# Expert rows fetched by indirect DMA and transposed, in place of one-hot products over a split copy of all tokens

## The chip, the core and the metric

The kernel runs on one core of a Trainium2 chip. The metric is the time of one execution on the device, in microseconds (us). A core has five engines that run their own instruction streams: TensorE (PE, matrix products; loading its stationary operand shows apart as PEld), VectorE (DVE), ScalarE (ACT), GpSimd (POOL) and SyncE (SP, which here only issues DMAs). Data moves between DRAM and the on-chip memory through 16 DMA engines that all queues share.

## The reference

The reference is a transformer-like block over 512 tokens of width 1024: RMS norm, an RWKV-7 mixer and a Mamba-2 mixer side by side, gates, an output projection `w_out` with a residual, then a mixture of experts and a last RMS norm. Only the mixture matters for this change:

```
h2 = rmsnorm(x, ffn_norm_g)
grp    = argmax(h2 @ w_rg + b_rg)                 # one of 4 groups
experts = top 2 of the 8 experts of that group    # 32 experts in all
hid = silu(h2[tok] @ w_gate[e]) * (h2[tok] @ w_up[e])
y[tok] += weight * (hid @ w_down[e])
out = rmsnorm(x + y, final_norm_g)
```

Each of the 32 experts has three float32 matrices of 2 MB. Every token goes to two experts, so there are 1024 token rows for all experts together.

## The kernel before

The mixers fill the first 1000 us or so and the change does not touch their code. After them comes the output projection, in eight steps `block(k)` / `turned(k)` of 128 columns. `turned` turns the result back to token rows, keeps it as `x2` (token in the partition) and also writes `th`: all tokens with the channel in the partition, split into a high part and a rest so that two fast products add up to full precision. The split takes one ACT pass and one DVE (once a POOL) pass per step. The last step is followed by the router: a chain of small DVE operations on the scores, with PE kept busy by 60 and then 24 transposes of the identity (`awake`).

The experts are taken in 8 groups of 4. An expert has 64 places (`CAP`), so a group has 256. `one_hot` compares, on DVE, each token's place with the 256 places of the group and so makes `oh` (second choice) and `sel` (both choices): a matrix of tokens against places. From it come three things on PE:

- `gather`: the group's token rows, channels in the partition (`xe`). For each of 8 channel pieces it multiplies `th` by `sel`: 4 token tiles times 2 parts, 8 products of 256 columns, 64 per group, and ACT copies each piece out of PSUM with the norm's gain.
- `scales`: the gate weights and norms of the places, 16 products of 4 columns each, read by DVE into `gsl`.
- `transposed`/`turned`: `sel` turned, for adding the results back (`combine`).

An expert is then `hidden` (16 products for gate and up, two column halves at a time; `between()` runs after the first 8), `turn` (4 transposes of the hidden values) and `down` (16 products), whose result ACT copies to `yy` and DVE splits. PE's order is written out by hand (`manual_schedule`), exactly as the loop over `groups` calls it: the next group's `one_hot` after its first expert, `scales` and `turned` after the second, the whole `gather` after the fourth. For group 0 the first half of the gather stands before the first expert, the second half in its `between()`, and `scales` after its `hidden`. The other engines' order follows from the order of the code by a scheduler.

Weights are read by `expert_weights`: six DMAs of 1 MB per expert, all on SP's queue, in the order gate, up, gate, up, down, down. They take 15 slots in turn (`wslot`): 2 in a pool that is free when the mixers end, 8 in one that is free soon after, 4 that take the memory of the projection's input, and 1 that opens after the router. A DMA into a used slot waits for the PE instruction that read the slot last, and the DMAs behind it on SP's queue wait with it.

At the end the last group is added, each of 4 token tiles is normalised and written out. Tokens beyond an expert's 64 places would run a loop at the end (`tc.If`); in the profiled execution it is not entered.

Of the kernel before, what the change touches and what calls it, by code (L numbers as in the profile page):

```python
# [17 lines left out]
T = 512  # L18
D = 1024
# [20 lines left out]
# TensorE's order in the two phases of streams: a letter is the next piece of that stream, a number before it  # L40
# how many pieces of projections come first
# [21 lines left out]
def hybrid_block(ctx: ExitStack, tc: tile.TileContext, a, out):  # L63
# [52 lines left out]
    # eye4[32 q + 8 d + h, i, c] = 1 where i = 4 c + d  # L116
# [42 lines left out]
    acs_d = dram.tile([SH, T], F32, name="acs_d")  # L159

# [552 lines left out]
    # twice the sigmoid is tanh + 1; the up projections are halved for it  # L713
# [6 lines left out]
    # gu takes acc in once both are gated  # L720
# [203 lines left out]
    gr = xp.tile([128, 2, TT, 2, 2], F32R, name="gr")  # L924
# [4 lines left out]
    th = xp.tile([128, 2, KT, TT, 128], F32R, name="th")  # L929
    NEXA, NEXB, NEXC, NEXD = 2, 8, 4, 1  # L930
# [24 lines left out]
    with tc.tile_pool(name="op", bufs=2, side="right") as op:  # L955
# [33 lines left out]
        def turned(k, xT):  # L989
# [22 lines left out]
            pk = ps.rearrange("p (t c k) -> p k t c", t=TT, k=KT)  # L1012
# [16 lines left out]
        # TensorE's clock stays up while the experts are chosen  # L1029
# [65 lines left out]
        gf = sm("gf", 2, TT, 2)  # L1095
        V.tensor_copy(gf[:, 0, :, 0], rst)
        G.memset(gf[:, 1, :, 0], 0.0)
# [16 lines left out]
    eps_ = moe.enter_context(tc.tile_pool(name="eps", bufs=1, space=PSUM))  # L1114
    sf = S0.rearrange("p e s -> p (e s)")
# [16 lines left out]

    def scales(o, sel, ne):
        pt = eps_.tile([128, 4, CAP], F32, name="pt", tag="pt", bufs=1)
        pf = pt.rearrange("p k c -> p (k c)")
        n = min(128, ne * CAP)
        gsl = mo.tile([128, EG], F32, name="gsl", tag="gsl", bufs=2)
        for p in range((ne + 1) // 2):
            for j, w in enumerate((sel, o)):
                for t in range(TT):  # L1140
                    PE.matmul(pf[0:n, 4 * p:4 * p + 4], w[:, t, 128 * p:128 * p + n],  # L1141
                              gr[:, j, t].rearrange("p i q -> p (i q)"), start=j == 0 and t == 0, stop=j == 1 and t == TT - 1)
        sc = mo.tile([128, 8], F32, name="sc", tag="sc")
        V.tensor_copy(sc[0:n, 0:4 * ((ne + 1) // 2)], pf[0:n, 0:4 * ((ne + 1) // 2)])
        for e in range(ne):
            rows, c = slice(64 * (e % 2), 64 * (e % 2) + 64), 4 * (e // 2)
            for i in range(2):
                V.tensor_tensor(gsl[64 * i:64 * i + 64, e:e + 1], pf[rows, c + i:c + i + 1], sc[rows, c + 2 + i:c + 3 + i], op=OP.add)
        return gsl
# [4 lines left out]
    def gather(sel, n, xe=None, ks=range(KT)):  # L1154
        if xe is None:
            xe = rows_tile(n)
        for k in ks:
# [5 lines left out]
        return xe  # L1163
# [7 lines left out]
    def hidden(group, ws, q, ss_, between=lambda: None):  # L1171
# [8 lines left out]
        if group.gsl is None:  # L1180
            group.scales()
# [44 lines left out]
    class Prepared:  # L1226
        def __init__(self, g):
            self.ne = groups[g]
            n = self.ne * CAP
            self.gsl = None  # L1230
            self.o, self.sel = one_hot(sf[:, 0:n], n, float(T * first_of[g]))

        def gather(self, ks):
            if ks[0] == 0:
                self.xe = rows_tile(self.ne * CAP)
            gather(self.sel, self.ne * CAP, self.xe, ks)

        def scales(self):
            self.gsl = scales(self.o, self.sel, self.ne)
# [16 lines left out]
    nxt.gather(range(KT // 2))  # L1256
# [12 lines left out]
    for g, ne in enumerate(groups):  # L1269
        cur, nxt = nxt, None  # L1270
        for q in range(ne):
            ws = expert_weights(first_of[g] + q)
            def between():
                if not pend:
                    cur.gather(range(KT // 2, KT))
# [11 lines left out]
            if g + 1 < len(groups):  # L1287
# [28 lines left out]
    # tokens past an expert's first CAP  # L1316
    most = nc.values_load(cnt[0:1, 0:1], min_val=0, max_val=2 * T)
    with tc.If(most >= CAP + 1):
        sx = mo.tile([128, CAP], F32, name="sx", tag="sx")
        V.tensor_scalar(sx, S0[:, 0], float(CAP), None, op0=OP.add)  # L1320
        with tc.For_i(0, NE, 1) as e:
# [8 lines left out]
            for b in range(1, T // CAP):  # L1330
                more = Overflow()
                more.o, sel = one_hot(sx, CAP, 0.0)
                more.gsl = scales(more.o, sel, 1)
                more.xe = gather(sel, CAP)
# [36 lines left out]
```

## Time and profile before

| | us |
|---|---|
| median of 3 runs | 1612.97 |
| lowest and highest run | 1611.62, 1616.58 |
| profiled execution, first to last instruction (span) | 1610.7 |
| PE busy in the span | 1512.8 (94%) |
| DVE, ACT, POOL busy | 906.0, 690.8, 236.5 |
| HBM read over the span | 298.60 MB |

The page gives no other time of the profiled execution than its span, which is 2.3 below the median of the runs. In the profile a line such as L1161 is a line of the kernel's file; a group of instructions is named by what it writes and reads (`gps<-sel,th` is the gather's product into a PSUM tile `gps`). PE's products overlap, so the mean of one is longer than the distance from one to the next. "ld" is the loading of the stationary operand.

### The profile page before, as it was taken

What the parts mean: (1) busy time and instruction counts of PE and PEld (TensorE: products, weight loads), DVE (VectorE), ACT (ScalarE), POOL (GpSimd) and SP (SyncE); (2) the same over time, 40 slices, a digit from 0 to 9 for tenths busy, and PEclk for the clock granted to TensorE, in tenths of its full rate; (3) what the DMA queues carried; (4) which work ended last, traced back from release to release, by engine and by line L of the source; (5) the groups of instructions that cost most, each with busy time, mean ns of one, the idle gap of its engine ahead of it and who ended that gap; (6) DMA issues with size and microseconds to landing.
All of it is one profiled execution on the core that took longest, in us unless ns stands there. A gap on an engine that the chain in (4) does not pass through costs nothing.

```text
span 1610.7 us, 22331 instructions
## 1 busy us (share of the span) xinstructions
PE 1512.8 (94%) x8510; PEld 1000.1 (62%) x8510; DVE 906.0 (56%) x1942; ACT 690.8 (43%) x1316; POOL 236.5 (15%) x223
## 2 busy tenths in 40 slices
PE   6988999999999999989898989999999999999995
PEld 5755766667766777767686767884454545544532
DVE  5688757887677845464565677434333343343334
ACT  6556566674746544545555654422221212212211
POOL 3122002220122000141313455000000000000001
PEclk9999999989999999999999999999999999999998
DMA  4321222212222323775655538749899999899991
GB/s 143 93 58 32 62 64 84 63 42 60 82 65 68 107 85 118 232 200 148 177 181 156 170 92 252 274 157 368 337 391 390 418 371 417 362 393 389 364 406 55
DMA packets 182612, 319.06 MB, mean 198 GB/s; under 512 B 10569, under 2 KB 141891, under 8 KB 156899
## 3 DMA queue, kind: packets, MB, share of 16 engines
q1 hardware_dynamic: 180131, 316.90, 55.2%
q8 instruction: 69, 1.13, 0.3%
q10 hardware_dynamic: 2368, 0.68, 0.2%
q14 instruction: 44, 0.36, 0.1%
HBM read 298.60 MB, written 18.94 MB: 197 GB/s over the span
## 4 chain that ended last, share of the span: by engine, by line
PE 52%; DMA 5%; DVE 4%; ACT 3%; POOL 2%; issue 2%; SPq 0%; ACTq 0%; DVEq 0%; POOLq 0%
PE pgu L1176 14%; PE pd L1201 7%; PE pin L150 5%; PE pin L152 5%; PE pin L151 5%; PE gps L1219 4%; PE gps L1161 4%; DMA er<-acs_d 2%; PE pt L1192 1%; DMA lt<-acs_d 1%; DMA gt<-g_d 1%; PE pt L1141 1%; DVE wl L135 1%; ACT wh L69 1%; POOL lt L796 1%
## 5 line engine op out<-in xcount | busy, mean ns | idle before, releaser
L150 PE MATMUL pin<-hh,wh 128*128 128x512 f32 x664 | 301.6, 454 | 11.7 <-ACT wh L69 7.7
L152 PE MATMUL pin<-hh,wl 128*128 128x512 f32 x664 | 271.6, 409 | 13.3 <-DVE wl L135 13.3
L151 PE MATMUL pin<-hl,wh 128*128 128x512 f32 x664 | 270.9, 408 | 0.8 <-DVE hl L229 0.8
L1176 PE MATMUL pgu<-we,xe 128*64 128x512 f32 x512 | 232.7, 597 | 0.0
L1177 PE MATMUL pgu<-we,xe 128*64 128x512 f32 x512 | 232.7, 597 | 0.0
L135 DVE TENSOR_TENSOR wl<-raw,wh 128x1024 fp32r<-128x1024 f32 x115 | 152.9, 1329 | 106.0 <-ACT wh L69 104.9
L69 ACT ACTIVATE wh<-raw 128x1024 fp32r<-128x1024 f32 x115 | 121.3, 1055 | 98.9 <-PE pin L151 82.0
L150 PEld LDWEIGHTS pin<-hh,wh 128*128 128x128 f32 x664 | 130.3, 196 | 49.6 <-issue 10.3
L152 PEld LDWEIGHTS pin<-hh,wl 128*128 128x128 f32 x664 | 129.8, 195 | 48.9 <-DVE wl L135 18.1
L151 PEld LDWEIGHTS pin<-hl,wh 128*128 128x128 f32 x664 | 131.1, 197 | 27.7 <-issue 5.3
L1176 PEld LDWEIGHTS pgu<-we,xe 128*64 128x64 f32 x512 | 66.1, 137 | 127.3 <-issue 123.9
L69 ACT ACTIVATE hid<-pgu,gsl 64x512 f32<-64x512 f32 x32 | 21.8, 681 | 280.4 <-PE pgu L1177 280.4
L1201 PE MATMUL pd<-we,hT 128*64 128x512 f32 x512 | 116.1, 593 | 1.2 <-DVE yy L1206 1.2
L1185 DVE SCALAR_TENSOR_TENSOR hid<-pgu,gsl,hid 64x512 f32<-64x512 f32 x32 | 24.2, 756 | 113.0 <-ACT hid L69 113.0
L150 PE MATMUL pin<-yh,wh 128*128 128x512 f32 x192 | 78.9, 411 | 7.5 <-ACT wh L69 3.3
L1201 PEld LDWEIGHTS pd<-we,hT 128*64 128x64 f32 x512 | 37.5, 137 | 73.8 <-issue 71.9
L1308 POOL TENSOR_SCALAR ss<-ss 128x1 f32<-128x1 f32 x4 | 2.4, 609 | 531.4 <-ACT y L69 531.4
L1221 DVE TENSOR_TENSOR x<-gps,x 128x512 f32<-128x512 f32 x128 | 78.1, 682 | 3.3 <-PE gps L1219 3.3
L1206 DVE TENSOR_TENSOR yy<-pd,yy 64x512 fp32r<-64x512 f32 x64 | 44.0, 687 | 63.4 <-ACT yy L69 62.5
L152 PE MATMUL pin<-yh,wl 128*128 128x512 f32 x192 | 76.7, 399 | 2.0 <-DVE wl L135 2.0
L69 ACT ACTIVATE yy<-pd 64x512 fp32r<-64x512 f32 x64 | 37.8, 591 | 89.8 <-PE pd L1201 88.9
L151 PE MATMUL pin<-yl,wh 128*128 128x512 f32 x192 | 76.1, 397 | 0.1
(365 smaller groups left out, 2675.8 us busy)
## 6 DMA issues: line engine op xcount, KB each, us to landing
we<-in_w_exp_gate_dram SPq DMA_DIRECT2D x64, 1024.0 KB
we<-in_w_exp_up_dram SPq DMA_DIRECT2D x64, 1024.0 KB
we<-in_w_exp_down_dram SPq DMA_DIRECT2D x64, 1024.0 KB
raw<-in_w_in_dram SPq DMA_DIRECT2D x83, 512.0 KB
lt<-acs_d SPq DMA_DIRECT2D x16, 512.0 KB
raw<-in_w_up_ssd_dram SPq DMA_DIRECT2D x16, 512.0 KB
xc_d<-cv SPq DMA_DIRECT2D x24, 256.0 KB
gt<-g_d SPq DMA_DIRECT2D x24, 256.0 KB
```

The costliest lines, as they stand in the source:

```text
L69: S.activation(o, i, f, **kw)
L135: V.tensor_tensor(lo, raw, hi.bitcast(F32), op=OP.subtract)
L150: PE.matmul(ps, wh[:, k, cs], xh[:, k], start=k == 0, stop=False)
L151: PE.matmul(ps, wh[:, k, cs], xl[:, k], start=False, stop=False)
L152: PE.matmul(ps, wl[:, k, cs], xh[:, k], start=False, stop=k == kt - 1)
L1161: PE.matmul(ps[:, 0:n], th[:, i, k, t], sel[:, t], start=i == 0 and t == 0, stop=i == 1 and t == TT - 1)
L1176: PE.matmul(pgu[0:64], xe[k // 4][:, k % 4, ss_], wg[k // 4][:, k % 4], start=k == 0, stop=k == KT - 1)
L1177: PE.matmul(pgu[SR], xe[k // 4][:, k % 4, ss_], wu[k // 4][:, k % 4], start=k == 0, stop=k == KT - 1)
L1201: PE.matmul(pd[i][64 * i:64 * i + 64], hT[:, k], wd[k // 2][:, k % 2, 512 * i:512 * i + 512], start=k == 0, stop=k == 3)
L1206: V.tensor_tensor(yy[i][rows, 1], src, yy[i][rows, 0].bitcast(F32), op=OP.subtract)
L1219: PE.matmul(ps, oT[0:n, 128 * t:128 * t + 128], yy[i][0:n, q], start=q == 0, stop=q == 1)
L1221: V.tensor_tensor(av, ps, av, op=OP.add)
```

## The change

The split copy `th` (32 KB per partition) is gone. In its place each step of the output projection writes its 128 columns of `x2` to a DRAM tensor `x2_d`, by a DMA on ACT's queue. `scales` multiplies by two more columns, of which one holds the token's number plus one, so that it yields for each place the token that sits there (or none). DVE turns that into an index list `at`. Two indirect DMAs on POOL's queue (`fetch`) then read the rows of 128 places each from `x2_d` into `xg`, one row of 4 KB per partition; places without a token have an index past the end and are left out. `gather` transposes `xg` on PE, 16 transposes of 128x128 per group in place of 64 products, and ACT copies as before. The memory of `th` becomes three more weight slots (`NEXA` 2 to 5, 18 in all) and the two `xg` tiles.

```diff
-    NEXA, NEXB, NEXC, NEXD = 2, 8, 4, 1
+    NEXA, NEXB, NEXC, NEXD = 5, 8, 4, 1
...
-            tk = [th[:, i, :, :, 16 * k:16 * k + 16] for i in range(2)]
-            act(tk[0], pk, AF.Copy)
             act(x2[:, :, ds_], ps.rearrange("p (t c) -> p t c", c=128), AF.Copy)
-            if k < KT - 1:
-                V.tensor_tensor(tk[1], pk, tk[0].bitcast(F32), op=OP.subtract)
-            else:
-                G.tensor_tensor(tk[1], x2[:, :, ds_].rearrange("p t (c k) -> p k t c", k=KT), tk[0].bitcast(F32), op=OP.subtract)
+            nc.scalar.dma_start(x2_d.rearrange("(t p) d -> p t d", p=128)[:, :, ds_], x2[:, :, ds_])
...
+        G.memset(gf[:, 1], 0.0)
+        G.iota(gf[:, 0, :, 2], pattern=[[128, TT]], base=1, channel_multiplier=1, allow_small_or_imprecise_dtypes=True)
...
+    xg = [mo.tile([128, D], F32, name=f"xg{p}") for p in range(2)]
+    for p in range(2):
+        G.memset(xg[p], 0.0)
...
+        tok = sc.rearrange("p (b q) -> p b q", q=6)[0:n, 0:np_, 2]
+        V.tensor_scalar(past[0:n, 0:np_], tok, 0.0, 4096.0, op0=OP.is_equal, op1=OP.mult)
+        V.scalar_tensor_tensor(at[0:n, 0:np_], tok, -1.0, past[0:n, 0:np_], op0=OP.add, op1=OP.add)
...
+    def fetch(at, ne):
+        n = min(128, ne * CAP)
+        for p in range((ne + 1) // 2):
+            G.indirect_dma_start(out=xg[p][0:n], out_offset=None, in_=x2_d,
+                                 in_offset=bass.IndirectOffsetOnAxis(ap=at[0:n, p:p + 1], axis=0),
+                                 bounds_check=T - 1, oob_is_err=False)
...
+    def gather(xe, ps_, n=128):
+        for k in range(KT):
             ps = ptile()
-            for i in range(2):
-                for t in range(TT):
-                    PE.matmul(ps[:, 0:n], th[:, i, k, t], sel[:, t], start=i == 0 and t == 0, stop=i == 1 and t == TT - 1)
-            act(xe[k // 4][:, k % 4], ps[:, 0:n], AF.Copy, scale=fgp[:, k:k + 1])
+            for i, p in enumerate(ps_):
+                PE.transpose(ps[:, n * i:n * i + n], xg[p][0:n].rearrange("p (c k) -> p k c", k=KT)[:, k], ident[0:n, 0:n])
+            act(xe[k // 4][:, k % 4, 128 * ps_[0]:128 * ps_[0] + n * len(ps_)], ps[:, 0:n * len(ps_)], AF.Copy,
+                scale=fgp[:, k:k + 1])
...
     nxt = Prepared(0)
-    nxt.gather(range(KT // 2))
+    nxt.fetch()
+    nxt.gather([0])
...
                 if not pend:
-                    cur.gather(range(KT // 2, KT))
+                    cur.gather([1])
                     return
...
                 if q == 1:
-                    nxt.scales()
+                    nxt.fetch()
                     nxt.turned()
                 if q == ne - 1:
-                    nxt.gather(range(KT))
+                    nxt.gather([0, 1])
```

On PE, between the router's `awake` (`rt<-ident`) and the first half of the first expert (`pgu`), the kernel before has the first half of the gather:

```order
L1033 MATMUL rt<-ident 128x128 x24
L1161 MATMUL gps<-sel,th 128x256 x32
L1176 MATMUL pgu<-we,xe 64x512
```

The changed kernel has the products of `scales` and then the transposes of the first fetched tile at that place:

```order
L1027 MATMUL rt<-ident 128x128 x24
L1140 MATMUL pt<-gr,sel 128x6 x4
L1140 MATMUL pt<-gr,oh 128x6 x4
L1140 MATMUL pt<-gr,sel 128x6 x4
L1140 MATMUL pt<-gr,oh 128x6 x4
L1170 MATMUL gps<-ident,xg_9375 128x128 x8
L1185 MATMUL pgu<-we,xe 64x512
```

So the 16 products of `scales`, the index list and a DMA now stand ahead of the first expert, where 32 products stood.

On POOL's queue, from the last operation of the output projection on, the kernel before has the last split of `th` and then nothing until the last norm (`ss`):

```order
L998 TENSOR_TENSOR rst<-rst,halfn 128x4
L1019 TENSOR_TENSOR th<-x_8729,th 128x32x16
L1308 TENSOR_SCALAR ss_12673<-ss_12673 128x1
```

The changed kernel has there two clears of `xg` and sixteen fetches, two per group, of which the first four are shown:

```order
L1112 MEMSET xg_9375 128x1024
L1112 MEMSET xg_9376 128x1024
L1158 DMA xg_9375<-x_d,at 128x1024
L1158 DMA xg_9376<-x_d,at 128x1024
L1158 DMA xg_9375<-x_d,at 128x1024
L1158 DMA xg_9376<-x_d,at 128x1024
```

The split left POOL, and the fetches have its queue to themselves.

On SP's queue, from the first weights of an expert on, the loads of `w_out` (`raw`) and of weights (`we`) stood in this order before:

```order
L951 DMA we<-in_w_exp_up_dram 128x2048
L131 DMA raw<-in_w_out_dram 128x8x128 x2
L951 DMA we<-in_w_exp_gate_dram 128x2048
L951 DMA we<-in_w_exp_up_dram 128x2048
L131 DMA raw<-in_w_out_dram 128x8x128
L951 DMA we<-in_w_exp_down_dram 128x2048
```

And they stand so in the changed kernel:

```order
L951 DMA we<-in_w_exp_up_dram 128x2048
L131 DMA raw<-in_w_out_dram 128x8x128
L951 DMA we<-in_w_exp_gate_dram 128x2048
L951 DMA we<-in_w_exp_up_dram 128x2048
L131 DMA raw<-in_w_out_dram 128x8x128
L951 DMA we<-in_w_exp_down_dram 128x2048
```

One load of `w_out` moved behind two loads of weights there; 14 weight loads are now in the queue ahead of the wait for the projection's last product, where 10 were.

## Rows read from the trace of the kernel before

**Rows 1.** The page: GB/s moved by DMA in 40 equal slices of the span.

```profile
GB/s 143 93 58 32 62 64 84 63 42 60 82 65 68 107 85 118 232 200 148 177 181 156 170 92 252 274 157 368 337 391 390 418 371 417 362 393 389 364 406 55
```

**Rows 2.** The page's DMA issues: what, queue, count, KB each.

```profile
we<-in_w_exp_gate_dram SPq DMA_DIRECT2D x64, 1024.0 KB
```

**Rows 3.** Windows: length, busy us (instructions) of PE, PEld, DVE, ACT, POOL, clock, DMA share, GB/s.

```profile
1300.00:1350.00 50.00, 50.00 (x263) 24.18 (x264) 18.32 (x40) 10.47 (x19) 0.00 (x0) 1.00 1.01 420
...
1450.00:1500.00 50.00, 50.00 (x267) 24.99 (x268) 16.64 (x35) 10.48 (x19) 0.00 (x0) 1.00 0.93 364
```

**Rows 4.** Chain of waits, 1075 to 1610, its longest pieces: start, us, what.

```profile
1328.29 7.86 PE gps L1161 x64
...
1521.51 7.86 PE gps L1161 x64
```

**Rows 5.** Waits of SP's queue, 960 to 1610: total us, times, longest.

```profile
SPq L951 <- PE pd L1201: 254.9, 50, 15.5
```

**Rows 6.** Waits of the engines, 1075 to 1610: total us, times, longest.

```profile
PEld pgu L1176 <- DMA we<-in_w_exp_down_dram: 0.7, 2, 0.4
```

**Rows 7.** Groups by line, 960 to the end: shapes, count, busy us, mean ns.

```profile
L1161 PE MATMUL gps<-sel,th 128*128 128x256 f32 x512 | 64.2, 285 | 0.2
...
L1192 PEld LDWEIGHTS pt<-ident,hid 64*128 64x128 f32 x128 | 17.7, 209 | 26.6 <-issue 25.1 <-PE pgu L1177 1.5
...
L69 ACT ACTIVATE xe<-gps,fgp 128x256 f32<-128x256 f32 x64 | 30.4, 475 | 34.8 <-PE gps L1161 34.7
```

**Rows 8.** Timeline at the gather of group 1: start, us, engine, line, what.

```profile
1135.02 7.93 PE L1161 MATMUL gps<-sel,th 128*128 128x256 f32 x64
1135.12 1.21 ACT L69 ACTIVATE yy<-pd 64x512 fp32r<-64x512 f32 x2 [2.73 <-PE pd L1201]
...
1142.88 0.64 PE L1176 MATMUL pgu<-we,xe 128*64 128x512 f32 x1
```

**Rows 9.** Timeline from the router to expert 0's scales.

```profile
1065.63 1.52 POOL L1019 TENSOR_TENSOR th<-x,th 128x512 fp32r<-128x512 f32 x1 [2.15 <-ACT x L69]
...
1066.08 1.21 DVE L1045 TENSOR_TENSOR f32A<-el,m 128x128 f32<-128x128 f32 x1
...
1068.94 0.29 DVE L1045 TENSOR_TENSOR f32A<-el,m 128x128 f32<-128x128 f32 x1
...
1074.83 0.88 DVE L1130 SCALAR_TENSOR_TENSOR sel<-S,idf,oh 128x256 fp32r<-128x256 f32 x2
...
1079.43 0.64 PE L1176 MATMUL pgu<-we,xe 128*64 128x512 f32 x1
...
1092.62 0.17 DVE L1144 COPY sc<-pt 128x8 f32<-128x8 f32 x1 [16.61 <-PE pt L1141]
```

**Rows 10.** Chain of waits, 950 to 1200: start, us, what.

```profile
976.44 2.75 DMA gt<-g_d
...
1083.09 4.03 PE gps L1161 x32
...
1090.70 1.89 PE pt L1141 x16
...
1107.27 0.95 PE gps L1168 x8
```

**Rows 11.** PE in short windows: length, PE busy (instructions), granted clock, DMA share, GB/s.

```profile
303.00:304.00 1.00, 0.00 (x0) 1.00 0.00 0
...
305.00:306.00 1.00, 1.00 (x5) 0.50 0.38 80
...
308.00:309.00 1.00, 1.00 (x5) 0.92 0.00 0
...
964.00:968.00 4.00, 2.10 (x10) 1.00 0.09 33
968.00:972.00 4.00, 3.26 (x15) 1.00 0.49 151
```

**Rows 12.** Groups of POOL over the whole span.

```profile
L534 POOL MEMSET TF<- 128x1024 f32 x8 | 8.3, 1043 | 109.0 <-PE cb L588 108.9
```

More of the change, by code (lines that the diff above doesn't have):

```diff
@@ L159, in hybrid_block @@
     acs_d = dram.tile([SH, T], F32, name="acs_d")
+    x2_d = dram.tile([T, D], F32, name="x2_d")
     x_in = a["x"][0]
@@ L923, in hybrid_block @@
     cnt = xp.tile([128, 1], I32, name="cnt")
-    gr = xp.tile([128, 2, TT, 2, 2], F32R, name="gr")
+    gr = xp.tile([128, 2, TT, 2, 3], F32R, name="gr")
     S0 = xp.tile([128, EG, CAP], F32, name="S0")
@@ L928, in hybrid_block @@
     nc.scalar.dma_start(fgp, a["ffn_norm_g"][0].rearrange("(p k) -> p k", k=KT))
-    th = xp.tile([128, 2, KT, TT, 128], F32R, name="th")
-    NEXA, NEXB, NEXC, NEXD = 2, 8, 4, 1
+    NEXA, NEXB, NEXC, NEXD = 5, 8, 4, 1
     ex = ctx.enter_context(tc.tile_pool(name="ex", bufs=NEXB, side="right"))
@@ L1135, in scales @@
         pf = pt.rearrange("p k c -> p (k c)")
-        n = min(128, ne * CAP)
+        n, np_ = min(128, ne * CAP), (ne + 1) // 2
         gsl = mo.tile([128, EG], F32, name="gsl", tag="gsl", bufs=2)
-        for p in range((ne + 1) // 2):
+        for p in range(np_):
             for j, w in enumerate((sel, o)):
                 for t in range(TT):
-                    PE.matmul(pf[0:n, 4 * p:4 * p + 4], w[:, t, 128 * p:128 * p + n],
+                    PE.matmul(pf[0:n, 6 * p:6 * p + 6], w[:, t, 128 * p:128 * p + n],
@@ L1142, in scales @@
                               gr[:, j, t].rearrange("p i q -> p (i q)"), start=j == 0 and t == 0, stop=j == 1 and t == TT - 1)
-        sc = mo.tile([128, 8], F32, name="sc", tag="sc")
-        V.tensor_copy(sc[0:n, 0:4 * ((ne + 1) // 2)], pf[0:n, 0:4 * ((ne + 1) // 2)])
+        sc = mo.tile([128, 12], F32, name="sc", tag="sc")
+        V.tensor_copy(sc[0:n, 0:6 * np_], pf[0:n, 0:6 * np_])
+        tok = sc.rearrange("p (b q) -> p b q", q=6)[0:n, 0:np_, 2]
+        past = mo.tile([128, 2], F32, name="past", tag="past")
@@ L1145, in scales @@
+        at = mo.tile([128, 2], I32, name="at", tag="at", bufs=2)
+        V.tensor_scalar(past[0:n, 0:np_], tok, 0.0, 4096.0, op0=OP.is_equal, op1=OP.mult)
+        V.scalar_tensor_tensor(at[0:n, 0:np_], tok, -1.0, past[0:n, 0:np_], op0=OP.add, op1=OP.add)
         for e in range(ne):
-            rows, c = slice(64 * (e % 2), 64 * (e % 2) + 64), 4 * (e // 2)
+            rows, c = slice(64 * (e % 2), 64 * (e % 2) + 64), 6 * (e // 2)
             for i in range(2):
-                V.tensor_tensor(gsl[64 * i:64 * i + 64, e:e + 1], pf[rows, c + i:c + i + 1], sc[rows, c + 2 + i:c + 3 + i], op=OP.add)
@@ L1149, in scales @@
-        return gsl
+                V.tensor_tensor(gsl[64 * i:64 * i + 64, e:e + 1], pf[rows, c + i:c + i + 1], sc[rows, c + 3 + i:c + 4 + i], op=OP.add)
+        return gsl, at
+    def fetch(at, ne):
[4 more added lines that the diff above has]
+                                 bounds_check=T - 1, oob_is_err=False)
@@ L1151, in rows_tile @@
     def rows_tile(n):
         return [wp.tile([128, KT // 2, n], F32, name="xe", tag="wh", bufs=2) for i in range(2)]
[L1154 to L1157, printed above, removed]
+    def gather(xe, ps_, n=128):
+        for k in range(KT):
             ps = ptile()
-            for i in range(2):
-                for t in range(TT):
-                    PE.matmul(ps[:, 0:n], th[:, i, k, t], sel[:, t], start=i == 0 and t == 0, stop=i == 1 and t == TT - 1)
-            act(xe[k // 4][:, k % 4], ps[:, 0:n], AF.Copy, scale=fgp[:, k:k + 1])
-        return xe
+            for i, p in enumerate(ps_):
+                PE.transpose(ps[:, n * i:n * i + n], xg[p][0:n].rearrange("p (c k) -> p k c", k=KT)[:, k], ident[0:n, 0:n])
+            act(xe[k // 4][:, k % 4, 128 * ps_[0]:128 * ps_[0] + n * len(ps_)], ps[:, 0:n * len(ps_)], AF.Copy,
+                scale=fgp[:, k:k + 1])
@@ L1179, in hidden @@
                 between()
-        if group.gsl is None:
-            group.scales()
         gsl = group.gsl[:, q:q + 1]
@@ L1229, in __init__, with fetch, gather @@
             n = self.ne * CAP
-            self.gsl = None
             self.o, self.sel = one_hot(sf[:, 0:n], n, float(T * first_of[g]))
-        def gather(self, ks):
-            if ks[0] == 0:
+        def fetch(self):
+            self.gsl, at = scales(self.o, self.sel, self.ne)
+            fetch(at, self.ne)
+        def gather(self, ps_):
+            if ps_[0] == 0:
                 self.xe = rows_tile(self.ne * CAP)
-            gather(self.sel, self.ne * CAP, self.xe, ks)
-        def scales(self):
-            self.gsl = scales(self.o, self.sel, self.ne)
+            gather(self.xe, ps_)
         def turned(self):
@@ L1332, in hybrid_block @@
                 more.o, sel = one_hot(sx, CAP, 0.0)
-                more.gsl = scales(more.o, sel, 1)
-                more.xe = gather(sel, CAP)
+                more.gsl, at = scales(more.o, sel, 1)
+                fetch(at, 1)
+                more.xe = rows_tile(CAP)
+                gather(more.xe, [0], CAP)
                 oT = turned_tile()
```

4 lines of the change are left out of this document (1 added, 3 removed).

## Prediction

> **What bounds the kernel now.** I read the page's slices first: from about 1080 us to the end PE is busy in every slice, at full clock, while DMA moves 360 to 420 GB/s [rows 1]. Two resources are thus near their limit, and the windows say which one leads: from 1300 to 1350 and from 1450 to 1500 PE is busy for 50.00 of 50 us, although the transfers ran at 420 GB/s in the one and at 364 in the other [rows 3]. PE sets the pace. The waits say it again: SP's queue, which issues the weights, waited 254.9 us for products that had yet to read a slot [rows 5], PE only 0.7 us for a weight [rows 6]. The chain of waits gives the period: two gathers that are three groups apart start at 1328.29 and 1521.51, so a group of four experts takes 193.22 / 3 = 64.41 us, of which the gather is one piece of 7.86 [rows 4]. In a period 24 loads of 1024 KB [rows 2] move 25.17 MB, that is 391 GB/s, against 420 where the queue was never out of slots [rows 3].
>
> So in this phase what leaves PE's stream comes off the time, until PE needs less per group than the transfers.
>
> **The gather of groups 1 to 7.** Removed are 64 products in 7.86 us of PE: the first product of the next expert comes at 1142.88, the gather began at 1135.02 [rows 8]. Added are 16 transposes of 128x128. The eight of L1168, of that shape, took 0.95 us [rows 10], 0.119 each, so PE itself needs 1.9 us; or 3.3 us if each is held by its stationary load read with a stride, as in L1192 (209 ns, at a smaller shape [rows 7]). But each pair fills a PSUM tile, there are three tiles, and ACT empties them with the copies it made before, 475 ns each [rows 7]. ACT is busy at that moment: two copies of `yy` run from 1135.12 for 1.21 us [rows 8], so its first copy of the gather starts at about 1136.35. The old products hid that; the transposes don't. With 0.49 us per copy (0.475 and a little between two), the eighth tile's transposes can start when the fifth copy has ended, at 1136.35 + 5 x 0.49 = 1138.8, and end at about 1139.1. The gather takes 4.1 us, and each group saves 3.7: 7 x 3.73 = **-26.1**. Bounds: if PE alone paced it, 5.9 saved per group, -41.7; if each copy costs 0.1 more for the hand-over between PE and ACT, a gather of 5.9 and 2.0 saved, -13.7. I take the middle value, which goes by the copies' own row.
>
> `scales` keeps its 16 products (six columns for four) and its place after the second expert, and `at` is ready some 26 us before the gather that uses it (one and a half experts of 16.1 us). A fetch of 0.5 MB has that long to land: nothing in groups 1 to 7, unless it is very late (a rival below).
>
> **The start, group 0.** Here nothing hides the fetch. Before: the two last `sel` tiles begin at 1074.83 and take 0.88, the gather's first half follows, and the first `pgu` starts at 1079.43 [rows 9]. After, step by step:
>
> - POOL's split at L1019 goes. Beside it one DVE step took 1.21 us, its like three steps later 0.29 [rows 9]: the router is 0.92 shorter and `sel` is done at 1074.8.
> - 13 of the 16 products of `scales` need the last `sel`: 13 x 1.89 / 16 [rows 10] = 1.5, to 1076.4.
> - DVE copies `sc`, makes `past` and `at`: three small steps of about 0.17 [rows 9] with hand-overs and what DVE has begun, together 1.2, to 1077.6.
> - POOL's two clears of `xg`, 1.04 each [rows 12], run beside the router's end; their cover is some 3 us, without it they cost up to 2.1.
> - The fetch. No indirect DMA is in this trace. Nearest is a direct load of 256 KB, 2.75 us from issue to landing [rows 10], against 256 KB of rows here. I take 3.5, to 1081.1; bounds 2 and 10.
> - Eight transposes and copies of 128 columns: ACT paces them, at most 0.475 less a little; 2.4 to the last copy that the first product wants.
>
> The first `pgu` comes at about 1083.5, +4.1. Given back: the gather's second half takes 2.4 in place of 4.03 (-1.6), and `scales` is gone from behind the first `hidden` (-1.9, both [rows 10]). That leaves +0.6. Then the clock: PE has nothing to do for some 5 us. [...] Some 3.5 us at half clock cost about 1.7. The start is **+2.3**; from -3 (short fetch, clock holds) to +10.
>
> **What costs nothing.** The removed ACT and DVE passes of the projection and the added writes of `x2_d` lie beside PE's products, which fill that stage; if the writes delayed it, it would be through their 2 MB of traffic, 5 us at 420 GB/s, beside transfers that have pauses there. I take 0, bounds -2 and +2. The order on SP's queue moves one load of `w_out` by two loads of weights; the same bounds. The last norm is untouched.
>
> **Does DMA keep up?** The fetches add 0.52 MB per group: 25.69 MB, 61.2 us at 420 GB/s, against 64.41 - 3.73 = 60.7 of PE. The two are level. The three added slots carry the difference: 18 loads are 45 us of transfers ahead of PE, of which about 25 are slots PE still reads (`down` is read an expert later), so about 20 us (an estimate) can be eaten over the phase, where 8 x 0.5 = 4 are needed. I take 0; without the slots it would be about +4.
>
> **Sum**, against the profiled execution (span 1610.7, the median of the runs 2.3 above): -26.1 + 2.3 = -23.8, a span of 1586.9 and a time of **1589**.
>
> [...] The row: a DVE step with two inputs in SBUF went from 0.29 to 1.21 us beside a POOL operation [rows 9]. [...]
>
> **The rivals.**
>
> *Deeper.* ACT's copies start at once or PE paces: -36 to -40, **1574**. For it: 1.9 us of PE's own work. Against: ACT's `yy` copies are in the way in each group. 0.08.
>
> *DMA becomes the bound.* The windows show 420 and 364, the latter with PE at 50 of 50 [rows 3], so it was waiting for slots, but nobody knows how much of it. If the sustained rate is 404, a group takes 63.6 us, 2.9 above PE; 8 x 2.9 - 20 = 3: **1592**. If 391 is all there is, 65.7, 8 x 5 - 20 = 20: **1609**. Against: 420 over 50 us. 0.17. [...]
>
> *The clock falls, or the start is long.* A fetch of 10 us or so at the start: +8, **1597**. Or the clock falls in every gather, since PE works for 1.9 of 4.1 us: 7 x 1.7 = 12, **1601**. Against the second: from 964 to 968 PE worked 2.10 of 4 us, and the clock stayed at 1.00 there and in the next 4 us [rows 11]. 0.15 together.
>
> *The fetch comes late, slower than before.* One mechanism: POOL makes the two fetches of a group slowly (row by row, or starved beside DVE, or in line behind 1 MB loads), and PE stands at the gather of each group until they land. From `at` to the gather there are 26 us; the gain of 24 is gone when a pair takes 26 + 24 / 7 = 29.4 us, and at 35 us it costs 7 x 9 = 63 less 24: **1652**. For it: no indirect DMA was seen here. Against: 256 KB took 2.75 us elsewhere [rows 10], ten times less. 0.07.
>
> *It doesn't do what it says:* transposes and copies in turn without overlap, 8 x (0.24 + 0.475 + hand-over) = 7 us and more, so the gather is as long as it was: about 0 and the start, **1614**. 0.06.
>
> **Numbers.** The forecast as described has 0.47. The range is 1577 to 1604: it takes in the bounds of the gather, the start and the milder half of DMA, and leaves out the deepest gain, 391 GB/s and the last two. A difference of 0.3%, 4.8 us, is what a measurement of this kernel can tell. Faster by more: forecast, deeper, clock and most of DMA, 0.86; within: part of DMA's, and of the last, 0.06; slower 0.08.
>
> **What would show it.** The gather on PE: about 4.1 us, waiting for `xe` copies, the first one behind `yy`. The distance between gathers of neighbouring groups: 60.7. The first `pgu` some 4 us later, with a granted clock of 0.5 shortly before or after it. Waits of PE for `xg` only at group 0. DMA at 0.95 to 1.0 with about 420 GB/s. I am wrong in the bound if PE waits for `we` by more than 5 us in all, in the fetch if any gather after group 0 waits for `xg`, and in the copies if the gather is under 3 or over 6 us.

## The result and the profile after

The changed kernel took 1595.68 us (median of 4 runs, 1592.07 to 1599.62), the kernel before 1614.78 in the runs beside it: a ratio of 0.9878, 95% interval 0.9847 to 0.9909. It is 19.1 us faster; 23.8 were forecast, and 1589 lies 6.7 below the time measured. The profiled execution has a span of 1590.4, 20.3 below the span before.

In the expert phase the same windows as in [rows 3] now read (length; busy us and instructions of PE, PEld, DVE, ACT, POOL; granted clock, DMA share, GB/s):

```profile
1300.00:1350.00 50.00, 49.07 (x226) 20.41 (x222) 20.53 (x37) 8.62 (x17) 1.59 (x2) 1.00 1.01 424
1450.00:1500.00 50.00, 50.00 (x236) 21.14 (x234) 19.51 (x40) 6.69 (x11) 1.99 (x2) 1.00 0.91 375
```

PE has short gaps now (0.93 us in the first window, one per gather; none in the second, which holds no gather). DMA moves 424 GB/s in the first, where it moved 420, and 375 in the second, where it moved 364; in the windows between them it is at 423 and 424. The gather of group 1, against [rows 8], in the timeline (start, us, engine, line, what; in brackets the idle time before it and what ended it):

```profile
1143.18 0.93 PE L1170 MATMUL gps<-ident,xg 128*128 128x128 f32 x6
1143.28 1.21 ACT L69 ACTIVATE yy<-pd 64x512 fp32r<-64x512 f32 x2 [2.73 <-PE pd L1208]
...
1144.52 3.03 ACT L69 ACTIVATE xe<-gps,fgp 128x256 f32<-128x256 f32 x8
1145.04 1.95 PE L1170 MATMUL gps<-ident,xg 128*128 128x128 f32 x10 [0.93 <-ACT xe L69]
1146.92 0.64 PE L1185 MATMUL pgu<-we,xe 128*64 128x512 f32 x1
```

Three pieces (six transposes) are done in 0.93 us, then PE waits for ACT, which copies `yy` until 1144.49 and only then the first piece. From 1143.18 to 1146.92 the gather takes 3.74 us, where it took 7.86. The last gather starts at 1504.98:

```profile
1504.98 0.93 PE L1170 MATMUL gps<-ident,xg 128*128 128x128 f32 x6
```

Six groups lie between them: (1504.98 - 1143.18) / 6 = 60.30 us per group, against 64.41.

The start looks worse than forecast. The timeline from the router to the first expert:

```profile
1068.78 6.71 PE L1027 MATMUL rt<-ident 128*128 128x128 f32 x60
...
1076.85 1.39 DVE L1127 TENSOR_SCALAR oh<-S,idf 128x256 fp32r<-128x256 f32 x2
1077.04 2.09 POOL L1112 MEMSET xg<- 128x1024 f32 x2 [8.19 <-DVE idf L1075]
...
1079.48 0.87 DVE L1128 SCALAR_TENSOR_TENSOR sel<-S,idf,oh 128x256 fp32r<-128x256 f32 x2
...
1082.82 0.16 DVE L1148 SCALAR_TENSOR_TENSOR at<-sc,past 128x2 int32<-128x2 f32 x1
...
1083.88 1.31 POOL L1158 DMA_INDIRECT xg<-x_d,at  x1 [4.74 <-DVE at L1148]
...
1087.62 2.66 PE L1170 MATMUL gps<-ident,xg 128*128 128x128 f32 x8 [5.61 <-DMA xg<-x_d,at]
...
1090.21 1.12 PE L1185 MATMUL pgu<-we,xe 128*64 128x512 f32 x1
```

Before, the router's keep-awake products began at 1064.22:

```profile
1064.22 7.55 PE L1033 MATMUL rt<-ident 128*128 128x128 f32 x60
```

The first `pgu` came at 1079.43 [rows 9], 15.21 us later; now it is 21.43.

And there is a loss ahead of the router that I had not forecast. In the first step of the output projection the waits of PE (total us, times, longest) show

```profile
PE plg L1000 <- DVE xT L986: 6.0, 1, 6.0
```

and the timeline of DVE, ACT's queue and SP's queue says why:

```profile
998.87 0.42 SPq L951 DMA_DIRECT2D we<-in_w_exp_up_dram  x1
...
1000.06 0.94 ACTq L970 DMA_DIRECT2D wr<-in_w_router_expert_dram  x1
...
1004.23 0.65 SPq L951 DMA_DIRECT2D we<-in_w_exp_down_dram  x1
...
1013.14 0.46 DVE L971 TENSOR_TENSOR wr<-wr,vec 128x288 f32<-128x288 f32 x1 [9.37 <-DMA wr<-in_w_router_expert_dram]
```

The router's weights `wr` (two small loads, whose rows are 16 and 128 bytes) need 13.1 us from issue until DVE can use them, while loads of 1 MB (`up` and `down` here, and a `gate` issued at 998.24) are on the engines with them. From 1004 to 1006 us the DMA view counts, for the queue of the weights (q1) and that of `wr` (q10), packets, MB and the share of the 16 engines:

```profile
q1 hardware_dynamic: 105, 0.80, 98.6%
q10 hardware_dynamic: 104, 0.00, 2.9%
```

In these 2 us the two queues get 105 and 104 packets through; for `wr`, which has 2080 (q10 from 998 to 1014), that is next to no bytes. `wr` stands on DVE ahead of the `xT` that PE waits for. The kernel before issued it at 1002.88, with its next expert weights only at 1007.75:

```profile
1007.02 1.01 DVE L971 TENSOR_TENSOR wr<-wr,vec 128x288 f32<-128x288 f32 x1 [0.44 <-DMA wr<-in_w_router_expert_dram]
```

There it took 4.1 us, and PE did not wait for it. The pause has a second price, the clock (1 us windows: length, PE busy and instructions, granted clock, DMA share, GB/s):

```profile
1012.00:1013.00 1.00, 0.00 (x0) 0.50 0.18 68
1016.00:1017.00 1.00, 1.00 (x6) 0.50 0.17 52
1019.00:1020.00 1.00, 1.00 (x6) 1.00 0.91 184
...
1084.00:1085.00 1.00, 0.00 (x0) 0.50 0.00 0
...
1092.00:1093.00 1.00, 1.00 (x6) 0.50 0.00 0
```

It falls to 0.50 in both pauses and stays there for 4 to 6 us after PE works again (from 1014.26 and from 1087.62); in [rows 11] it was nearly as long.

The first product of the projection stands so before and in the changed kernel:

```profile
1001.85 0.48 PE L150 MATMUL pin<-mh,wh 128*128 128x512 f32 x1
...
999.29 0.48 PE L150 MATMUL pin<-mh,wh 128*128 128x512 f32 x1
```

Stage by stage, from these rows and [rows 4, 8, 9]:

| stage | before | after | difference |
|---|---|---|---|
| to the first product of the projection (1001.85; 999.29) | | | -2.6 |
| from there to the router's keep-awake products | 62.37 | 69.49 | +7.1 |
| to the first `pgu` | 15.21 | 21.43 | +6.2 |
| to the first `pgu` of group 1 (1142.88; 1146.92) | 63.45 | 56.71 | -6.7 |
| six more groups | 6 x 64.41 | 6 x 60.30 | -24.7 |
| the rest | | | +0.3 |

The sum is -20.4, of a measured -20.3. The first line is no work of the change: that product starts between 993.95 and 1005.48 in the profiles of all kernels of this study, whose code up to there is the same but for where slots and `wr` are taken.

### The profile page after: what moved, and what is told of

It reads as the page before. It is cut to its first block, busy times and chain, and to the rows that moved or that the text cites. A ratio compares the mean times of both kernels' runs of the same rounds, so it can differ in the third digit from the quotient of the medians.

```text
span 1590.4 us, 21601 instructions
## 1 busy us (share of the span) xinstructions
PE 1472.9 (93%) x8126; PEld 954.3 (60%) x8126; DVE 901.8 (57%) x1951; ACT 683.4 (43%) x1316; POOL 256.2 (16%) x241
## 5 line engine op out<-in xcount | busy, mean ns | idle before, releaser
L1158 POOL DMA_INDIRECT xg<-x_d,at x16 | 16.2, 1012 | 387.2 <-DVE at L1148 384.8
```

Source lines behind the costliest of these rows:

```text
L1158: G.indirect_dma_start(out=xg[p][0:n], out_offset=None, in_=x2_d, in_offset=bass.IndirectOffsetOnAxis(ap=at[0:n, p:p + 1], axis=0), bounds ...
```

## The experiments

Ratios are to the kernel before, with 95% intervals; in the same terms the changed kernel has 0.9878 (0.9847 to 0.9909).

**1. The router's weights early.** Theory W: the projection is late because `wr` shares the DMA engines with weight loads that the new order lets in ahead of it. Rivals: the writes of `x2_d`; or a gain that is given back.

```diff
+    wr = mp.tile([128, KT, 36], F32, name="wr")
+    nc.scalar.dma_start(wr[:, :, 0:4], ...)     # beside mh, ml, some 32 us earlier
+    nc.scalar.dma_start(wr[:, :, 4:36], ...)
...
-        wr = op.tile([128, KT, 36], F32, name="wr", bufs=1)
```

> The changed kernel with the two loads of the router's weights (wr, packets of 16 and 128 B) issued some 30 to 40 us earlier, into memory that is free then; nothing else is moved but their place on ACT's queue. Theory W (in the changed kernel wr shares the DMA engines with 1 MB weight loads that the new slots let in earlier, so it takes 12.7 us from issue to landing where it took 4.1 before, PE stands for 6.0 us in the first projection step and then works some 4 us at half clock): the wait of DVE for wr (9.4 us) and the PE wait of 6.0 us go, the keep-awake products of the router start at 1061 in place of 1068.8, and the time falls by 6 to 8 us, to about 1588. Rival X (the projection is late because of the x2_d writes on ACT's queue or the slots' semaphores, and wr only happened to be waited for): the router starts at 1067 to 1069 as before, time within 2 us of the changed kernel. Rival Y (gained there, lost later: fewer of the 18 slots are full when the experts start): the router starts at 1061 but PE then waits for weights by 5 us or more in all.

Measured: 1589.52 us, 0.9828 (0.9791 to 0.9865). The wait is gone: the projection takes 62.31 us to the keep-awake products (1001.67 to 1063.98), as before the change. So W holds, and the writes of `x2_d`, which are still there, together with the passes that are gone come to nothing in the projection. But of the 7.2 us gained 4 came back in the router of this profile, which is neither of the rivals: it starts at half clock, as a 1 us window shows.

```profile
1063.00:1064.00 1.00, 1.00 (x7) 0.50 0.00 0
```

and the timeline of PE and DVE:

```profile
1063.98 8.96 PE L1027 MATMUL rt<-ident 128*128 128x128 f32 x60
...
1073.17 0.48 DVE L1074 TENSOR_TENSOR A<-A,rt 128x128 f32<-128x128 f32 x2 [2.71 <-PE rt L1071]
```

The 60 keep-awake transposes take 8.96 us here and 6.71 in the changed kernel's profile; the router's products stand behind them, and DVE waits 2.71 us. Whether the clock falls in the pause of 1.5 to 2 us at the end of the projection differs from one profile to the next (from 1063 to 1065 it is 0.50 in the kernel before, after a wait of 1.50 us; in the changed kernel's profile it is 1.00 in every window of 1 us from 1062 to 1083, with a wait of 1.45), and with it the time. It may be one source of the 7 us between the runs of one kernel; each kernel has one profile, so this is not shown.

**2. Fifteen slots.**

```diff
-    NEXA, NEXB, NEXC, NEXD = 5, 8, 4, 1
+    NEXA, NEXB, NEXC, NEXD = 2, 8, 4, 1
```

> The changed kernel with NEXA 2 in place of 5, so 15 weight slots as before the change. If the three slots carry the difference between DMA and PE (25.69 MB per group in 60.3 us would be 426 GB/s, the profile shows 424): PE waits for weights by 3 to 6 us in all and the time rises by about 4 us in the expert phase. If 15 slots are cushion enough: PE waits for weights under 2 us, the distance between gathers stays 60.3. Theory W says in addition: if the loads of gate and up no longer stand beside wr, the wait of PE for the first xT (6.0) shrinks; their order on SP's queue here is gate and up after two loads of w_out, so I expect 0 to 3 us of it.

Measured: 1589.51 us, 0.9829 (0.9797 to 0.9861), the same gain as experiment 1 from taking the slots away again. The distance of the gathers is 60.30 and the longest wait for weights in the phase 0.4 us: the three slots carried nothing. What they cost at the start shows in the timeline of SP's queue, ACT's queue and DVE:

```profile
1001.05 6.36 SPq L131 DMA_DIRECT2D raw<-in_w_out_dram  x2
...
1003.30 0.59 ACTq L970 DMA_DIRECT2D wr<-in_w_router_expert_dram  x1
...
1006.92 0.45 DVE L971 TENSOR_TENSOR wr<-wr,vec 128x288 f32<-128x288 f32 x1
...
1008.52 0.34 SPq L951 DMA_DIRECT2D we<-in_w_exp_gate_dram  x1
```

Two loads of `w_out`, the second of which waits, stand ahead of `gate` and `up` here (1008.52), so no load of 1 MB is issued between `wr` and its use, and DVE has it 3.6 us after its issue. I had expected the stall to shrink by 0 to 3 us; all 6 went. With 15 slots `xg` also lies in other memory, and POOL clears it at 971 us; with 18 it lies where the router's tiles were, and the clear waits for the last of them (8.19 us in the rows above). From the projection's first product to the first `pgu` it takes 81.47 us, against 90.92.

**3. The clears on ACT.**

```diff
-        G.memset(xg[p], 0.0)
+        act(xg[p], x2[:, 0], AF.Copy, scale=0.0)
```

> The changed kernel with the two clears of xg done by ACT (copies with scale 0) in place of POOL. Theory P (POOL's clears start when the last of idf is made and run beside DVE's first one-hot pieces, which take 0.69 us each there and 0.30 otherwise, so sel is 0.9 us late): the four oh pieces take 0.3 each, from the start of the router's keep-awake products to the first pgu it takes 20.5 in place of 21.4 us, the time falls by about 1 us (below what the runs can tell). Rival: the oh pieces are slow for their own reasons (first use) and stay at 0.69; no change.

Measured, in the timeline of DVE and ACT:

```profile
1084.00 0.62 DVE L1127 TENSOR_SCALAR oh<-S,idf 128x256 fp32r<-128x256 f32 x2
1084.01 2.00 ACT L69 ACTIVATE xg<-x 128x1024 f32<-128x1024 f32 x2 [0.69 <-DVE idf L1075]
```

The first two `oh` pieces take 0.62 us beside ACT's clears, 1.39 beside POOL's: theory P holds, 0.77 us. The 20.5 us that I expected for the start were not seen (22.47): DVE waits 2.35 us for the router's products in this profile, as it did in experiment 1 (2.71) behind keep-awake products at half clock. Which clock they had here is not shown; the mean over the span is 0.961, against 0.968 in the changed kernel's profile. Time 1598.00, 0.9889 (0.9854 to 0.9924): the same as the changed kernel, as a gain of 0.8 must look in such runs.

**4. PE kept at work while the fetch is under way (18 slots).**

```diff
     nxt.fetch()
+    ps = ptile()
+    for i in range(50):
+        PE.transpose(ps[:, 0:128], ident, ident)
     nxt.gather([0])
```

> The changed kernel with 50 transposes of the identity on PE (0.093 us each, 4.6 us) between the first scales and the first transposes of fetched rows, while PE waits for the first fetch. Theory C (the idle 5.6 us let the clock fall to half, and the first four pairs of gate and up products then take 1.06 us in place of 0.59): clock 1.00 from 1082 on, the first half of expert 0 takes 3.6 in place of 5.2 us, and the time falls by 1.6 to 2.2 us. Rival: the clock falls all the same, or PE's extra work delays the first transposes; no gain. The fetch itself should take as long as before: 3.7 us from POOL's start to PE's first transpose.

The time was 1601.26, 0.9885 (0.9841 to 0.9928): no gain, and theory C as I put it fell. The 1 us windows ahead of the fetch and at its start:

```profile
1090.00:1091.00 1.00, 0.52 (x2) 1.00 0.00 0
1091.00:1092.00 1.00, 0.59 (x4) 1.00 0.00 0
1093.00:1094.00 1.00, 1.00 (x6) 0.50 0.00 0
```

The timeline of the added transposes:

```profile
1093.77 8.37 PE L1266 MATMUL gps<-ident 128*128 128x128 f32 x50
```

The clock was at half before the added transposes began (1093.77): the last products of `scales` ahead of them, from 1092.91, take 0.99 us for four, in place of 0.59 in the changed kernel. So the 50 took 8.37 us (45 take 5.08 at clock 1.00 in experiment 8, 0.113 each), and PE's order puts them ahead of the gather. Which pause let the clock fall is not shown. PE had waited for `sel` a little earlier, 0.18 and 0.65 us, but the changed kernel waits there too (0.32 and 0.65), and its clock is still at 1.00 in the products of `scales`.

**5. Two pieces in one PSUM tile, in turns.** Theory G: PE waits in the gather for PSUM that ACT has yet to empty.

```diff
-            ps = ptile()
+            if k % 2 == 0:
+                bank = ptile()
+            ps = bank[:, 256 * (k % 2):256 * (k % 2) + 256]
```

> The changed kernel with two channel pieces in one PSUM tile (512 columns in place of 256), so that six of the eight pieces can be transposed before the first must be copied out; three tiles as before. Theory G (the gather's 3.74 us are PE waiting for PSUM that ACT empties, first behind two yy copies): the gather takes 2.6 to 2.9 us, PE's wait for xe copies (0.9 per group) goes, the distance between gathers is 59.2 to 59.5. Theory D (DMA is level with PE: 25.69 MB per group at 424 GB/s are 60.6 us): with 18 slots the difference of 1.3 us per group is still covered, so the time falls by 6 to 7.5 us and PE's waits for weights stay under 4 us. Rival: DMA already sets the pace, the distance stays at 60.3 and PE waits for weights by what the gather gave.

> The same gather with 15 slots. If the three more slots are what lets DMA keep up, PE waits here for weights by 3 to 8 us more than with 18 slots and the distance between late gathers is 60 or more. If 15 are enough: distance 59.2 to 59.5 in every group, waits for weights under 3 us, and a time about 1582 (1589.5 of the 15-slot kernel less 7). I expect the second, since the weights' period and PE's differ by only 1.3 us per group, 9 in all, and 15 slots hold 37 us of transfers.

Both were far off: 1638.84 us, 1.0162 (1.0122 to 1.0201) with 18 slots and 1627.60, 1.0094 (1.0057 to 1.0131) with 15, slower than the kernel before. PE in the gather of group 1 with 18 slots (timeline), and the window of 1 us behind it:

```profile
1147.99 0.49 PE L1172 MATMUL gps<-ident,xg 128*128 128x128 f32 x2
1149.85 0.71 PE L1172 MATMUL gps<-ident,xg 128*128 128x128 f32 x4 [1.37 <-ACT xe L69]
...
1155.00 1.12 PE L1188 MATMUL pgu<-we,xe 128*64 128x512 f32 x1
```

```profile
1155.00:1156.00 1.00, 1.00 (x5) 0.50 1.05 434
```

The second piece of a tile waits until ACT has read the first (PE waits 1.37, 0.70, 0.70 and 0.57 us for `xe` copies), so PE and ACT take turns. The gather takes 7.0 us; towards its end the clock is 0.84 (1152 to 1153) and behind it 0.50, and the next expert's first products take 1.06 to 1.12 us in place of 0.59; the gathers are 64.7 to 65.8 us apart. This is the last rival of the prediction (transposes and copies in turn), and with the clock of the third: it was real, it just isn't what the change does.

**6. No transposes in groups 1 to 7.**

```diff
         for k in range(KT):
+            if len(ps_) == 2:
+                to = xe[k // 4][:, k % 4]
+                if k % 2:
+                    act(to, x2[:, 0, 0:256], AF.Copy)
+                else:
+                    V.tensor_copy(to, x2[:, 0, 0:256])
+                continue
```

> The changed kernel (18 slots) without the transposes of groups 1 to 7: in their place ACT and DVE write xe from other data in SBUF, four pieces each; the fetches stay. Leaves out the gathering itself for those groups. PE has about 56.6 to 57 us of work per group, DMA 60.6 at 424 GB/s. Theory D: DMA becomes the bound once the cushion is eaten (I estimated about 20 us of 8 x 3.8 = 30): the late groups are 60 to 61 us apart, PE waits for weights by 8 to 15 us in all, the time falls by 10 to 17 us. Rival (DMA can do more than 424 GB/s or PE alone is the bound): all groups 56.6 to 57 apart, time 24 to 26 us shorter, waits under 4 us.

1583.34 us, 0.9808 (0.9761 to 0.9855), 12 below the changed kernel, though 3.9 us less of PE in seven groups would be 27. PE's longest group of waits (total us, times, longest), and two windows with the columns of the first fence:

```profile
PEld pgu L1193 <- DMA we<-in_w_exp_up_dram: 13.1, 9, 2.3
```

```profile
1200.00:1250.00 50.00, 50.00 (x238) 20.80 (x234) 21.53 (x48) 9.19 (x17) 2.11 (x2) 1.00 1.01 424
1400.00:1450.00 50.00, 47.13 (x218) 18.44 (x216) 20.03 (x46) 9.53 (x18) 2.11 (x2) 1.00 1.01 424
```

The first groups are 56.4 us apart with PE at 50.00 of 50; from about 1340 on PE waits for weights, with DMA at 424 GB/s in both windows, and the last two distances are 60.3 and 61.6. So theory D holds: 424 GB/s is what DMA gave here (421 to 425 in the windows of 50 us from 1150 to 1500), 25.69 MB take 60.6 us, and the changed kernel's 60.30 lies on that line. What PE saved beyond it came out of the stock of loaded weights.

**7. Every fetch twice (15 slots).**

```diff
-        for p in range((ne + 1) // 2):
+        for p in 2 * list(range((ne + 1) // 2)):
```

> The kernel with 15 slots, every fetch issued twice (32 in place of 16; POOL's queue and the traffic of the fetches doubled, 26.2 MB per group). What I said of the fetch (it has some 26 us to land): the gathers of groups 1 to 7 still wait for no xg, distances stay at 60.3 unless weights fall behind (61.8 us per group at 424 GB/s against 60.3, 12 us over the phase: with 15 slots I expect PE to wait for weights by 0 to 6). At the start the second pair delays the first transposes by about two POOL instructions, 1.3 + 1.0 and the gaps, 2.5 to 3.2 us. Time 1592 to 1598. Rival (late fetch, POOL starved or slow): gathers wait for xg in every group and the time is 1610 or more.

1597.48 us, 0.9885 (0.9853 to 0.9916), 8 above the kernel with 15 slots. The only wait of PE for `xg`:

```profile
PE gps L1170 <- DMA xg<-x_d,at: 8.9, 1, 8.9
```

PE waits for `xg` once, at group 0, 3.9 us longer than with single fetches (5.0); no later gather waits, and the distances are 60.30 until weights fall short in the last two groups (62.2 and 67.9, 9.4 us more in all, where 0 to 6 were expected). The rival of the late fetch is ruled out with room to spare: even twice the fetches land in time.

**8. A start without pauses, and pairs.** Three kernels, each with what the one before it has. The first has 15 slots and keeps PE at work:

```diff
                 act(sq, xT, AF.Square)
                 ps = rtile()
+                for t in range(20):
+                    PE.transpose(ps[:, 128:256], ident, ident)
...
     nxt.fetch()
+    nxt.turned()                      # moved from behind expert 0
+    ps = ptile()
+    for i in range(45):
+        PE.transpose(ps[:, 0:128], ident, ident)
     nxt.gather([0])
```

> The kernel with 15 slots with three things at the start that keep PE at work, and no other change: 20 transposes of the identity while it waits for the square of the last xT, the eight transposes of group 0's sel moved ahead of the first gather, and 45 transposes of the identity behind them while it waits for the first fetch. Theory C (the clock falls where PE pauses, and at half clock the router's keep-awake products and the first gate and up products take twice as long): clock 1.00 from 1060 to the end of expert 0, first half of expert 0 in 3.6 us, against the 15-slot kernel -1.6 (clock) and -1.0 (turned): time 1586 to 1588, and the runs differ by less than the 7 us of the changed kernel. Rival: it falls all the same, as it did with 50 transposes and 18 slots, where PE had paused 1 us in the 3 us before; then 1588 to 1592.

1584.00 us, 0.9822 (0.9788 to 0.9856). No window of 1 us from 1000 us to the end of expert 0 has a clock below 1.00; one of them, in the wait for the fetch:

```profile
1079.00:1080.00 1.00, 0.87 (x8) 1.00 0.36 135
```

From the first `pgu` to that of group 1 it takes 53.9 us in place of 56.0 with 15 slots alone: 0.9 of the 2.1 is the first half of expert 0 (3.6 us, at clock 1.00, in place of 4.5), the rest goes with the moved transposes of `sel` (1.09 us). So with PE kept at work in all three places the clock holds, as C says; what each of them does alone is not tested. The runs still differ by 13 us, from 1580.74 to 1594.23; what does that is open.

The second adds pairs: all eight transposes of two pieces into a tile, then both copies.

```diff
-        for k in range(KT):
-            ps = ptile()
+        for k2 in range(KT // 2):
+            ps = ptile()
+            for k in (2 * k2, 2 * k2 + 1):
...
+                    PE.transpose(ps[:, c:c + n], ...)
+            for k in (2 * k2, 2 * k2 + 1):
+                act(xe[k // 4]..., ps[:, w * (k % 2):w * (k % 2) + w], AF.Copy, scale=fgp[:, k:k + 1])
```

> The same, and the gather's pieces in pairs: eight transposes of two pieces into one PSUM tile, then two copies, so no copy reads a tile that PE still writes (as it did in the kernels in which PE and ACT took turns on one tile, with 7.0 us per gather). Theory G (three PSUM tiles are what holds PE in the gather): six pieces are transposed before the first copy is needed; the gather takes 2.6 to 3.0 in place of 3.74, the distance between gathers is 59.2 to 59.6, time 6 to 8 us below the run before it. DMA needs 60.6 per group at 424 GB/s, so with 15 slots I expect 0 to 4 us of waits for weights in the last two groups. Rival: the turn-taking is in any tile that holds two pieces; the gather takes 5 us or more.

1579.62 us, 0.9792 (0.9756 to 0.9827), the shortest time of the study. Its gather in the timeline, and the wait of PE for weights:

```profile
1134.03 1.60 PE L1175 MATMUL gps<-ident,xg 128*128 128x128 f32 x12
...
1136.26 0.72 PE L1175 MATMUL gps<-ident,xg 128*128 128x128 f32 x4 [0.62 <-ACT xe L69]
1136.90 0.64 PE L1191 MATMUL pgu<-we,xe 128*64 128x512 f32 x1
```

```profile
PE pgu L1192 <- DMA we<-in_w_exp_up_dram: 1.5, 1, 1.5
```

Theory G holds: six pieces go through before PE waits, and the gather takes 2.87 us. The groups are 59.43 apart until the last, 62.1, where the weights fall short. The time is 4.4 us below the run before it, not 6 to 8: of the 6.1 us that seven shorter gathers give, 2.7 go in that last group.

The third has 18 slots again, without what they did at the start as far as experiments 1 and 3 know it:

> The same as the one before it with 18 slots, the router's weights loaded early and the clears of xg on ACT, so that what the slots did to the start is gone as far as it is known. If the three slots are worth something once PE needs 59.4 us per group: waits for weights in the last groups 0 against 1 to 4 us with 15 slots, and a time 1 to 4 us shorter. If 15 were enough: the same within 2 us, or longer by what the start loses.

1583.49 us, 0.9797 (0.9763 to 0.9831). All groups are 59.4 apart, so the slots do give back the 2.7 us of the last group; but from the projection's first product to the first `pgu` it takes 84.48 us, against 81.58, and the clock falls once more in the fetch (0.50 at 1089). The two cancel. The loss is on POOL's queue:

```profile
1083.57 1.31 POOL L1160 DMA_INDIRECT xg<-x_d,at  x1 [17.17 <-DVE sel L1130]
```

`at` is ready at 1079.75, but by the trace POOL waits for a `sel` of the next group and starts the fetch 3.8 us later, where it took 0.3 with 15 slots. Why the fetch waits for that step is not shown.

## Why the prediction was right, step by step

**The bound, and the gather** were right. PE set the pace, and what left its stream came off. The forecast of 4.1 us per gather by ACT's copies behind `yy` is 3.74: the first copy came at 1.34 us, as worked out from [rows 8] (1.33), but the copies follow each other at 3.03 / 8 = 0.38 us, not 0.49. The copies overlap on ACT: the mean duration of one (475 ns in [rows 7], 488 in the changed kernel) is longer than their distance. The term is -28.8 for -26.1. Its bound of -13.7 does not follow from its premise: 0.1 us more on each copy makes a gather of 4.6 to 4.9 us, not of 5.9.

**The start** was forecast at +2.3 and is +3.5: +6.2 to the first `pgu`, +1.6 for the first half of expert 0 at half clock (5.21 us for eight pairs, 3.59 before; forecast 1.7), -1.8 for the second half of the gather and -1.9 for `scales` (forecast -1.6 and -1.9), and -0.6 for a wait of PE for `hid` that is gone. Within it three steps were off. From the end of `sel` to `at` it took 2.63 us (forecast 2.7), but the cover of the clears was no cover: they wait for the router's `idf` (8.19 us in the rows above; with 15 slots, where `xg` lies elsewhere, they do not), and cost DVE 0.77. From `at` to PE it took 4.64 us, forecast 3.5: 3.74 from POOL's start, in the middle of the range taken from [rows 10], and 0.9 before it. In the kernel with 15 slots POOL starts 0.3 after `at`; what the other 0.6 are I don't know. The split that left POOL did give its 0.92: L1039 takes 0.29 at both places. The forecast's 3.5 us at half clock, from which the 1.7 came, agree with the kernel before: its windows of 1 us from 304 to 309 have the clocks 0.87, 0.50, 0.50, 0.50 and 0.92, which makes 3.4 us at half clock; in the changed kernel the clock stayed at half for 5.9 us after PE's return, from 1087.62 to about 1093.5, the transposes of the first tile among them.

**"What costs nothing"** is the step that failed. It priced the order on SP's queue at 0, bounds -2 and +2, as one load of `w_out` that moves by two loads of weights. The runs put +7.1 there (by the windows of that stretch PE stood for 7.8 us, 2.1 before, and worked for 61.7, 60.3 before, partly at half clock): the loads moved in beside another queue's small transfer, `wr`, whose place had not changed. The writes and the removed passes, the other half of that step, are together 0 as said (experiments 1 and 2).

**Does DMA keep up** was right: 60.6 us per group at 424 GB/s against PE's 60.3, and the level is where the kernel now stands. But that the three slots carry the difference was wrong. 15 are enough at 60.3 us per group, and the +4 that I gave for a kernel without them is about -6.

Of the rivals, the DMA bound lies 0.3 us per group away and shows as soon as PE is faster (experiment 6); the late fetch is out (experiment 7); the clock did not fall in the gathers of 3.74 us (1.00 in every window of 50 us from 1100 to 1550), but did with a gather of 7.0 us (0.50, experiment 5). With the measured terms -28.8 + 3.5 + 7.1 the change is worth -18.2, the forecast was -23.8, and the gather's error hid a part of the projection's: that the time came this near to the forecast is in part luck.

## What to carry to other kernels

More buffers were not free here: the three slots changed which loads were in flight early, and `wr`, a small load on another queue that someone waits for, took 13.1 us beside them in place of 4.1. So look at each small transfer in the stretch where the added loads begin. The place of a tile decided the start of its clear as well: POOL's clear of `xg` waited 8.19 us for the router's `idf` with 18 slots and ran at 1077, with 15 it ran at 971. When PE's cut reaches the level of the transfers (60.3 us per group against 60.6), count the stock of loaded weights: in experiment 6 the late groups fell back to 60.3 and 61.6 us, because that stock was all that the further cut could be paid from.

## What was not expected of the hardware

- A load of rows of 16 and 128 bytes is in use 4.1 us after its issue in the kernel before and 3.6 us in experiment 2, where no load of 1 MB is issued between it and its use; in the changed kernel, with three such loads about it, 13.1 us. In 2 us of that time (1004 to 1006) its queue got 104 packets through and the queue of the weights 105, which were 0.00 and 0.80 MB.
- An indirect DMA of a tile with about half of its 128 rows of 4 KB in use (16 of them move 4.20 MB) holds POOL for 1.0 to 1.3 us. At group 0 of the changed kernel, with no weights under way (DMA share 0.00 from 1083 to 1085), PE uses it 3.7 us after POOL begins it. In the later groups, beside the weights, it takes longer (us from issue to landing), which is still within the 26 us that it has:

```profile
DMA to landing us min/median/max: 4.0/8.8/10.9
```

- The transfers of this phase reach 424 GB/s and stay at 418 to 424 over 300 us (1150 to 1450 of the changed kernel), with weights and fetched rows together.
